# A GLA layer and MLP on one core: units of their own for the last tiles of x, the rows of r brought back at once, x1 and the out weights loaded behind them

## The chip, the cores and the metric

The kernel runs on one core of a Trainium2 chip. The metric is the device time of one execution in microseconds (us). The core has five engines that run side by side and wait for each other by semaphores: PE (TensorE, matrix products), DVE (VectorE), ACT (ScalarE), POOL (GpSimd) and SP (SyncE), which here only issues transfers between the memory and the core (DMA). Each engine, and SP's queue of transfers, takes its instructions in order.

## The reference

With DEPTH = 1 only the first layer is run: gated linear attention (GLA) and an MLP, on 1024 tokens of 1024 numbers.

```python
x = x + gla_mixer(rms_norm(x, norm_mix), w_in, w_gk_up, b_gk, g_onorm, w_out)
x = x + sqrelu_mlp(rms_norm(x, norm_ffn), w_ff1, w_ff2)
return rms_norm(x, final_norm)

def gla_mixer(h, ...):
    q, k, v, r, gk_low = split(h @ w_in)
    log_a = log_sigmoid(gk_low @ w_gk_up + b_gk) / 16
    # per head and chunk of tokens: a state S, decayed by exp(cumsum(log_a))
    #   o = (q * exp(b)) @ S + tril(q k^T decayed) @ v ;  S = decay * S + k_dec^T v
    o = rms_norm(o, g_onorm)
    return (o * silu(r)) @ w_out
```

## The kernel before

Every float32 number is split in a high and a low part, and every product is done as three matmuls (`mm3`). The large products (x by the weights of q and k, of v, of r; the gated outputs by w_out; the MLP's two) go by Strassen's scheme in Winograd's form: seven half-size products ("steps", n = 0 to 6) of sums of 512x512 blocks instead of eight, 48 matmuls each.

The stage that matters is the one behind the q, k, v and r products: a loop over c = 0 to 7, the eight chunks of 128 tokens. PE's order is written out by hand (`manual_schedule`); ACT, DVE, POOL and SP get theirs from a planner that simulates the program and puts in all semaphores. For PE an iteration c is: the operands of chunk c+1 (`operands`, L618), one part of r's last products (`r_part`, L769), the chunk's outputs (`outputs`, L681), its contribution to the state (`new_state`, L652), and the transposes of the previous chunk's gated outputs (`outputs_T`, L709). Between outputs and transposes ACT and DVE normalise and gate the chunk (squares at L696, scale by the rows of r at L705).

r's product has two of its seven steps (n = 1 and 3, `R_LAST`) left out of the large stage for tokens 512 to 1023. They are done here instead, as eight parts `R_PARTS` = (4,1), (4,3), (5,1), ... (7,3), part c in iteration c, 12 matmuls each. The first of a token tile's two parts takes a new bank of PSUM (`rbank`), the second goes on in it. Each part needs:

- the split weights `wr[n]`, made once (L833) and kept in four `big` tiles;
- one tile of split x, 512 KB, brought back from the DRAM copy `xv` by `load_xt` (L755) in two transfers of 256 KB;
- the row tile `rr[t]` with the part of r that is already there. The r stage writes it to the DRAM tensor `rw` (L747, from staging tiles in `raw` and `g4`); `load_r` (L764) brings it back. DVE adds the part (L780), then ACT and DVE apply silu (L725 to L728).

Tiles come from pools with a fixed number of buffers. A new tile takes a buffer that is free, or waits for one. Those that are touched: `big` (8 buffers of 8 KB a partition), `raw` (2 of 4 KB), `wb` (4 of 4 KB), `vx` (8 of 4 KB). `wb` holds weight units in the large stages; in the chunk loop the split rows of v (`v_split`, L640, two tiles a chunk, free when `new_state` of that chunk is done) and the x tiles of `load_xt`. `raw` holds staging in the r stage (its last use there is step n = 4), nothing in the chunk loop, and sums for the out product behind it. `vx` holds v until `v_split`, then x1 (the residual) and one block of w_out.

Behind the loop comes the product with w_out: `from_out` (L904) loads its four blocks, each of two units of 512 KB (block 11 into `vx`, 21 into `wb`, 12 and 22 into `wa`); `load_x1` (L927) loads eight tiles of x, onto which the products are added (`onto_x1`, L931, DVE at L935). In the code before, x1's loads wait for v's last rows to be written (`last_v`), and the w_out loads for nothing but buffers.

`order_after(..., wait=False)` only tells the planner to put one instruction behind another; on one queue that costs no semaphore. `run(True)` (`general`) is a second form of the program for other inputs; it is behind a branch that is not taken here.

Of the kernel before, what the change touches and what calls it, by code (L numbers as in the profile page):

```python
# [8 lines left out]
F32 = mybir.dt.float32  # L9
F32R = mybir.dt.float32r  # L10
# [6 lines left out]
P = 128  # L17
T = 1024
# [22 lines left out]
def order_after(tc, inst, other, wait=True):  # L41

    kind = mybir.DependencyClass.Sync if wait else mybir.DependencyClass.NoSync
    tc.add_manual_dep(inst.ins, other.ins.name, mybir.DependencyInfo(kind, mybir.DependencyReason.DATA),
                      reason="order of phases")
# [3 lines left out]
def hybrid_trunk(ctx: ExitStack, tc: tile.TileContext, x, xT, w_head, w_r, w_gk, w_up,  # L49
                 w_out, w_ff1, w_ff2, vecs, g_fin, out):  # L50
    nc = tc.nc
# [8 lines left out]
    def new(tag, dtype=F32):  # L60
        count[0] += 1
        pool_ = ps if tag in ("mm", "gl") else sb
        return pool_.tile(SHAPE.get(tag, [P, 1024]), dtype, tag=tag, bufs=BUFS[tag], name=f"{tag}{count[0]}")
# [4 lines left out]
    def mm(o, w, m, start, stop, partial=False):  # L68

        pe.matmul(o, w, m, start=start, stop=stop, skip_group_check=partial)  # L70
# [48 lines left out]
    def run(general):  # L119
# [8 lines left out]
        def half(hf):  # L128
            return slice(hf * 512, hf * 512 + 512)
# [12 lines left out]
        R_FIRST, R_LAST = (0, 5, 2, 4, 6), (1, 3)  # L142
# [287 lines left out]
        box = {}  # L430
# [187 lines left out]
        def operands(c, bank_tag="gl"):  # L618

            ah, kd = (new("wa", F32R) for _ in range(2))  # L620
            hs, ls = slice(0, 512), slice(512, 1024)
            if general:
                for pair in range(2):
                    src = at_general[c // 4, pair].rearrange("p (h c t) -> p h c t", h=2, c=4)[:, :, c % 4, :]
                    split(two(ah[:, hs], pair), two(ah[:, ls], pair), src)
            else:
                dp = new(bank_tag)
                for h in range(H):
                    kc, qc = (qk_view(n, h)[:, c * P:c * P + P] for n in (1, 0))
                    mm(dp[:, h * P:(h + 1) * P], kc, qc, True, True)  # L630
                at = new("at")
                dve.tensor_tensor(chunks(at), chunks(dp), bc(cmask, [P, 4, P]), op=ALU.mult)
                split(ah[:, hs], ah[:, ls], at)
            kp = new(bank_tag)
            for h in range(H):
                pe.transpose(kp[:, h * P:(h + 1) * P], qk_view(1, h)[:, c * P:c * P + P], ident)  # L636
            split(kd[:, hs], kd[:, ls], kp)
            ops_c[c] = ah, kd

        def v_split(c):  # L640

            vh = [new("wb", F32R) for _ in range(2)]
            for pair in range(2):
                split(vh[pair][:, 0:512], vh[pair][:, 512:1024], v[c][:, half(pair)])
            v[c] = vh
# [35 lines left out]
        def outputs(c):  # L681

            ah = ops_c[c][0]
            S = state.get("S")
            on, st = new("g4"), new("st")
            ss, y, m, t2 = (st[:, 4 * n:4 * n + 4] for n in range(4))
            o = [new("gl") for _ in range(2)]
            for h in range(H):
                d = o[h // 2][:, (h % 2) * DV:(h % 2) * DV + DV]
                mm3(d, *hl_of(ah, h, P), *hl_of(v[c][h // 2], h % 2, DV), True, c == 0)  # L690
                if c:
                    mm(d, qk_view(0, h)[:, c * P:c * P + P], S[:, h * DV:h * DV + DV], False, True)
            with tc.high_priority():
                for h in range(H):
                    vs = slice(h * DV, h * DV + DV)
                    act.activation(on[:, vs], o[h // 2][:, (h % 2) * DV:(h % 2) * DV + DV], AF.Square, accum_out=ss[:, h:h + 1])  # L696
                act.activation(y, ss, AF.Ln, scale=r_ss[:, c:c + 1], bias=eps)
                act.activation(y, y, AF.Exp, scale=-0.5)
                dve.tensor_scalar(m, ss, r_ss[:, c:c + 1], EPS, op0=ALU.mult, op1=ALU.add)
                dve.tensor_tensor(t2, y, y, op=ALU.mult)  # L700
                dve.scalar_tensor_tensor(t2, t2, -0.5, m, op0=ALU.mult, op1=ALU.mult)
                dve.scalar_tensor_tensor(y, t2, 1.5, y, op0=ALU.add, op1=ALU.mult)
                for h in range(H):
                    vs = slice(h * DV, h * DV + DV)
                    dve.scalar_tensor_tensor(on[:, vs], o[h // 2][:, (h % 2) * DV:(h % 2) * DV + DV], y[:, h:h + 1],  # L705
                                             rr[c][:, vs], op0=ALU.mult, op1=ALU.mult)
            normed_o[c] = on
# [12 lines left out]
        rr, rbank, xt_, wr, stage = {}, {}, {}, {}, {}  # L720
# [33 lines left out]

        def load_xt(t, n):  # L755

            u = new("wb", F32R)
            u3 = u.rearrange("p (k c) -> p k c", c=P)
            for kh in range(2):
                src = xv[n][kh].rearrange("p (k t) -> p k t", t=512)  # L760
                nc.sync.dma_start(u3[:, 4 * kh:4 * kh + 4, :].bitcast(F32), src[:, :, (t % 4) * P:(t % 4) * P + P])
            xt_[t, n] = u3

        def load_r(t):  # L764

            rr[t] = new("big")
            nc.sync.dma_start(rr[t][:, 0:T], rw[t])

        def r_part(t, n):  # L769

            if n == R_LAST[0]:
                rbank[t] = new("mm")
            u, p_ = xt_.pop((t, n)), rbank[t]
            for kp in range(4):
                w = wr[n][kp // 2][:, kp % 2]
                mm3(p_, u[:, 2 * kp, :], u[:, 2 * kp + 1, :], w[:, 0, :], w[:, 1, :], n == R_LAST[0] and kp == 0,
                    n == R_LAST[1] and kp == 3, True)
            d = rr[t][:, half(int(PART[n][0]) - 1)]
            with tc.high_priority():
                dve.tensor_tensor(d, p_, d, op=ALU.add)  # L780
            silu(t, d, d, rr[t][:, T:T + 512])
# [48 lines left out]
        def r_last():  # L830

            for n in R_LAST:
                wr[n] = wR.split(n)  # L833
                load_xt(4, n)
            load_r(4)

        fine_steps.add((0, 0))
# [23 lines left out]
        last_v = box["v"]  # L861


        load_r(0)
        v_split(0)
        R_PARTS = [(t, n) for t in range(4, TT) for n in R_LAST]
        if not general:
            v_split(1)
        for c in range(TT):
            if c == 4 and not general:  # L870

                over = new("st")
                dve.tensor_reduce(over[:, 0:1], top, axis=mybir.AxisListType.X, op=ALU.max)
                dve.tensor_scalar(over[:, 1:2], over[:, 0:1], RANGE, None, op0=ALU.is_gt)
                pf = new("gl")
                mm(pf[:, 0:1], ones, over[:, 1:2], True, True)
                dve.tensor_copy(flag, pf[:, 0:1])
            more = c + 1 < TT
            if general:
                if c % 4 == 0:  # L880
                    for h in range(H):
                        prep_general(h, c // 4)
                operands(c)
                if c:
                    v_split(c)
            elif more:
                operands(c + 1, "mm")
                if c:
                    v_split(c + 1)
            if more:  # L890
                if c:
                    load_xt(*R_PARTS[c + 1])
                if c + 1 < 4:
                    load_r(c + 1)
                if R_PARTS[c + 1][1] == R_LAST[0]:
                    load_r(R_PARTS[c + 1][0])
            r_part(*R_PARTS[c])
            outputs(c)
            if more:
                new_state(c)  # L900
            if c:
                outputs_T(c - 1)

        def from_out(a, b, kh, dst):  # L904

            nc.sync.dma_start(dst.rearrange("p (h n) -> p h n", h=2),
                              w_out[4 * b + 2 * a:4 * b + 2 * a + 2, :, half(kh)].rearrange("h p n -> p h n"))

        def from_up(c):
            def bring(a, b, kh, dst):  # L910
# [14 lines left out]
        x1 = {}  # L925

        def load_x1(t):  # L927
            x1[t] = new("vx")
            order_after(tc, nc.sync.dma_start(x1[t], x[t * P:(t + 1) * P, :]), last_v)

        def onto_x1(n, lane, p_):  # L931
            e, dh = int(PART[n][0]) - 1, int(PART[n][1]) - 1
# [6 lines left out]

        so = Side(True, {f"{a}{b}": og_block(a, b) for a in (1, 2) for b in (1, 2)}, dve, pair_temp, late=True)  # L940
        wo = weight_side(False, from_out, dve, "vx")
        wo.load("11")
        wo.load("21")
        ops = [[so.split(0), wo.split(0)]]
        for t in range(4):
            load_x1(t)
        wo.load("12")
        wo.load("22")
        for t in range(4, 8):
            load_x1(t)  # L950
# [197 lines left out]
```

## Time and profile before

| | us |
|---|---|
| median of three runs | 1015.25 |
| the three runs | 1014.17, 1015.25, 1015.42 |
| the profiled execution | 1014.16 |
| its span | 1012.4 |
| mean granted clock of PE | 0.994 |

Times in the profile count from the start of the span; the span is 1.76 us shorter than the execution's own time. A row of a timeline gives start, duration (both us), engine, line, operation, output<-inputs, size, how many were merged, and in brackets how long the engine was idle before and what released it. PE is matmuls, PEld their weight loads, SPq the issuing of transfers by SP. A row of waits gives the total in us, how often, and the longest. A row of stretches gives length, then busy time (and count) of PE, PEld, DVE, ACT and POOL, the clock granted to PE, the DMA engines' busy share and GB/s. A row of transfers gives the count, the size of one and the median us from issue to landing. The chunk loop lies between about 227 and 308 us.

### The profile page before, as it was taken

Reading aid. Unit: us, or ns where it says so; the run is one execution under the profiler, and the core shown is the slowest. Engines: PE = TensorE matmul, PEld = TensorE weight load, DVE = VectorE, ACT = ScalarE, POOL = GpSimd, SP = SyncE. Lnnn points to the kernel's source line nnn. Section 1 sums busy time; section 2 is a strip of 40 time slices with the busy share of each in tenths; the row PEclk is TensorE's granted clock in tenths of the full one; section 3 lists DMA queues with packets and bytes.
Section 4 is the critical chain, followed back from the end, with each engine's and each line's share of the span. In section 5 each row is a group of like instructions: output and inputs, shape, how many; then the busy total and the mean of one; then the engine's idle time right before and its main releaser. Section 6 shows DMA issues by size and latency. Waiting matters only on the chain.

```text
span 1012.4 us, 12293 instructions
## 1 busy us (share of the span) xinstructions
PE 993.0 (98%) x4572; PEld 829.0 (82%) x4572; DVE 738.3 (73%) x899; ACT 555.9 (55%) x842; POOL 225.1 (22%) x142
## 2 busy tenths in 40 slices
PE   9999999999989999999999999999999999999995
PEld 8888878888878888888888888888888888888884
DVE  6994786868889998979964339965339965339965
ACT  7776555778775378667332446332446332446355
POOL 0000110113430000042224241224241224241270
PEclk9999999999999999999999999999999999999998
DMA  9899794576462224772224951124861124860004
GB/s 281 313 328 371 268 308 181 214 254 204 160 203 89 63 63 187 277 274 73 62 63 167 343 237 43 54 72 166 317 262 46 49 76 166 331 235 16 1 1 170
DMA packets 98957, 176.87 MB, mean 175 GB/s; under 512 B 5576, under 2 KB 67144, under 8 KB 87368
## 3 DMA queue, kind: packets, MB, share of 16 engines
q1 hardware_dynamic: 98328, 175.59, 48.9%
q8 instruction: 38, 0.62, 0.2%
q10 hardware_dynamic: 560, 0.40, 0.1%
q14 instruction: 31, 0.25, 0.1%
HBM read 138.23 MB, written 37.75 MB: 174 GB/s over the span
## 4 chain that ended last, share of the span: by engine, by line
PE 81%; DMA 2%; ACT 1%; DVE 1%; issue 1%; ACTq 0%; DVEq 0%
PE gl L70 54%; PE mm L70 26%; DMA wb<-xv 2%; PE mm L970 1%; DVE vx L935 0%; ACT g L1040 0%; PE mm L636 0%; PE mm L715 0%; ACT hq L717 0%; ACT st L1041 0%; ACT g L696 0%; DVE st L1044 0%; ACT big L81 0%; ACT st L1042 0%; DVE g L1048 0%
## 5 line engine op out<-in xcount | busy, mean ns | idle before, releaser
L70 PE MATMUL gl<-big,big 128*128 128x512 f32 x2712 | 631.3, 390 | 0.0
L70 PEld LDWEIGHTS gl<-big,big 128*128 128x128 f32 x2712 | 508.4, 188 | 105.1 <-DVE big L82 0.4
L70 PE MATMUL mm<-big,big 128*128 128x512 f32 x1224 | 288.2, 389 | 0.0
L70 PEld LDWEIGHTS mm<-big,big 128*128 128x128 f32 x1224 | 229.8, 188 | 47.7
L82 DVE TENSOR_TENSOR big<-wa,big 128x1024 fp32r<-128x1024 f32 (+1 forms) x120 | 162.0, 1376 | 105.4 <-ACT big L81 105.3
L81 ACT ACTIVATE big<-wa 128x1024 fp32r<-128x1024 f32 (+1 forms) x120 | 120.7, 1039 | 134.7 <-PE gl L70 64.0
L184 POOL TENSOR_TENSOR wa<-wa,wa 128x1024 f32<-128x1024 f32 x28 | 75.2, 2690 | 160.5 <-DVE big L82 159.6
L184 POOL TENSOR_TENSOR wa<-wa,wb 128x1024 f32<-128x1024 f32 x14 | 42.9, 3065 | 283.1 <-DVE big L82 283.1
L82 DVE TENSOR_TENSOR big<-wb,big 128x1024 fp32r<-128x1024 f32 x48 | 63.5, 1339 | 52.8 <-ACT big L81 50.6
L82 DVE TENSOR_TENSOR big<-hq,big 128x1024 fp32r<-128x1024 f32 x48 | 61.3, 1283 | 42.8 <-ACT big L81 42.8
L81 ACT ACTIVATE big<-wb 128x1024 fp32r<-128x1024 f32 x48 | 49.1, 1052 | 64.8 <-PE mm L70 31.0
L81 ACT ACTIVATE big<-hq 128x1024 fp32r<-128x1024 f32 x48 | 48.6, 1053 | 61.4 <-PE gl L70 32.4
L81 ACT ACTIVATE big<-raw 128x1024 fp32r<-128x1024 f32 x42 | 43.6, 1058 | 52.1 <-DVE raw L184 25.2
L82 DVE TENSOR_TENSOR big<-raw,big 128x1024 fp32r<-128x1024 f32 x42 | 66.8, 1607 | 2.3 <-ACT big L81 2.2
L935 DVE TENSOR_TENSOR vx<-gl,vx 128x512 f32<-128x512 f32 x95 | 63.2, 682 | 3.5 <-PE gl L70 3.2
L184 POOL TENSOR_TENSOR wa<-wb,wa 128x1024 f32<-128x1024 f32 x14 | 41.1, 2947 | 44.7 <-DVE big L82 44.7
L556 POOL COPY top<-g 128x4 f32<-128x4 f32 x8 | 8.5, 1066 | 179.7 <-DVE g L548 179.7
L993 ACT ACTIVATE hq<-hq 128x1024 f32<-128x1024 f32 x24 | 25.4, 1058 | 29.6 <-DVE hq L986 29.6
L678 POOL TENSOR_SCALAR g<-g,est 128x256 f32<-128x256 f32 x28 | 28.7, 1039 | 57.0 <-DVE g L675 37.8
L70 PE MATMUL gl<-wb,wa 128*128 128x256 f32 x180 | 32.5, 312 | 0.0
L70 PE MATMUL mm<-big,wb 128*128 128x512 f32 x96 | 25.3, 414 | 6.4 <-DMA wb<-xv 5.8
L935 DVE TENSOR_TENSOR vx<-mm,vx 128x512 f32<-128x512 f32 x45 | 29.8, 681 | 1.4 <-PE mm L70 1.4
(191 smaller groups left out, 834.0 us busy)
## 6 DMA issues: line engine op xcount, KB each, us to landing
big<-xw SPq DMA_DIRECT2D x42, 1024.0 KB, 6.8
big<-xv SPq DMA_DIRECT2D x20, 1024.0 KB, 5.7
xv<-big SPq DMA_DIRECT2D x14, 1024.0 KB, 8.1
xw<-big SPq DMA_DIRECT2D x14, 1024.0 KB, 5.5
wb<-in_w_ff SPq DMA_DIRECT2D x32, 256.0 KB, 3.3
wa<-in_w_ff SPq DMA_DIRECT2D x32, 256.0 KB, 3.7
wa<-in_w_ff SPq DMA_DIRECT2D x16, 512.0 KB, 4.6
wb<-in_w_ff SPq DMA_DIRECT2D x16, 512.0 KB, 4.5
```

What stands on the lines that cost most here:

```text
L70: pe.matmul(o, w, m, start=start, stop=stop, skip_group_check=partial)
L81: last["split"] = act.activation(hi, src, AF.Copy)
L82: last["low"] = dve.tensor_tensor(lo, src, f32(hi), op=ALU.subtract)
L184: op = self.eng.tensor_tensor(*(self.ap(b, kp, 2) for b in (o, x_, y_)), op=op)
L556: pool.tensor_copy(top[:, 8 * h + 4 * hf:8 * h + 4 * hf + 4].unsqueeze(2), a[:, :, P - 1:P])
L678: pool.tensor_scalar(S[:, vs], Z[:, vs], g, None, op0=ALU.mult)
L935: return dve.tensor_tensor(xd, p_, xd, op=ALU.add)
L970: pe.transpose(p_[:, c * P:(c + 1) * P], xn[4 * hf + c][:, kt * P:(kt + 1) * P], ident)
L993: act.activation(d2, d2, AF.Relu)
```

## The change

The x tiles get `raw`'s two buffers instead of `wb`'s. The rows of tokens 0 to 511 share two `big` tiles and are all brought back before the loop, the row of tile 5 with them; those of tiles 6 and 7 follow in iterations 2 and 4. The loads of w_out are put behind the load of part 6's x tile, and those of x1 behind part 7's, without a semaphore; x1's wait for v is gone.

```diff
         def load_xt(t, n):
-            u = new("wb", F32R)
+            u = new("raw", F32R)
...
-                nc.sync.dma_start(u3[:, 4 * kh:4 * kh + 4, :].bitcast(F32), src[:, :, (t % 4) * P:(t % 4) * P + P])
+                box["xt", t, n] = nc.sync.dma_start(u3[:, 4 * kh:4 * kh + 4, :].bitcast(F32),
+                                                    src[:, :, (t % 4) * P:(t % 4) * P + P])
...
         def load_r(t):
-            rr[t] = new("big")
+            if t >= 4 or t % 2 == 0:
+                box["rr"] = new("big")
+            rr[t] = box["rr"] if t >= 4 else box["rr"][:, (t % 2) * T:(t % 2) * T + T]
             nc.sync.dma_start(rr[t][:, 0:T], rw[t])
...
             for n in R_LAST:
                 wr[n] = wR.split(n)
-                load_xt(4, n)
+                if n == R_LAST[0] or not general:
+                    load_xt(4, n)
             load_r(4)
...
-        load_r(0)
+        for t in range(4):
+            load_r(t)
+        load_r(5)
         v_split(0)
...
             if more:
-                if c:
+                if c or general:
                     load_xt(*R_PARTS[c + 1])
-                if c + 1 < 4:
-                    load_r(c + 1)
-                if R_PARTS[c + 1][1] == R_LAST[0]:
-                    load_r(R_PARTS[c + 1][0])
+                if c in (2, 4):
+                    load_r(5 + c // 2)
             r_part(*R_PARTS[c])
...
         def from_out(a, b, kh, dst):
-            nc.sync.dma_start(dst.rearrange("p (h n) -> p h n", h=2),
+            load = nc.sync.dma_start(dst.rearrange("p (h n) -> p h n", h=2),
                               w_out[4 * b + 2 * a:4 * b + 2 * a + 2, :, half(kh)].rearrange("h p n -> p h n"))
+            order_after(tc, load, box["xt", 7, R_LAST[0]], wait=False)
...
         def load_x1(t):
             x1[t] = new("vx")
-            order_after(tc, nc.sync.dma_start(x1[t], x[t * P:(t + 1) * P, :]), last_v)
+            order_after(tc, nc.sync.dma_start(x1[t], x[t * P:(t + 1) * P, :]), box["xt", 7, R_LAST[1]], wait=False)
```

## The prediction

> **What bounds the kernel now.** I begin with the page's busy line and the list of what TensorE (PE) waited for, cut to the stage that the change touches (225 to 320 us).
>
> ```profile
> PE 993.0 (98%) x4572; PEld 829.0 (82%) x4572; DVE 738.3 (73%) x899; ACT 555.9 (55%) x842; POOL 225.1 (22%) x142
> ```
>
> ```profile
> PE mm L70 <- DMA wb<-xv: 5.8, 4, 2.8
> PE mm L70 <- ACT hq L717: 0.5, 1, 0.5
> ```
>
> PE is the bound: it is idle for 1012.4 - 993.0 = 19.4 us of the span. Here it waits 5.8 us, in four waits, for a load of x tiles. The timeline of PE shows where; these are all the gaps that it marks from 205 to 312 us:
>
> ```profile
> 245.70 2.96 PE L70 MATMUL mm<-big,wb 128*128 128x512 f32 x12 [0.86 <-DMA wb<-xv]
> 256.42 3.04 PE L70 MATMUL mm<-big,wb 128*128 128x512 f32 x12 [0.98 <-DMA wb<-xv]
> 277.67 3.03 PE L70 MATMUL mm<-big,wb 128*128 128x512 f32 x12 [1.15 <-DMA wb<-xv]
> 287.95 3.02 PE L70 MATMUL mm<-big,wb 128*128 128x512 f32 x12 [0.46 <-ACT hq L717]
> 299.26 4.19 PE L70 MATMUL mm<-big,wb 128*128 128x512 f32 x12 [2.85 <-DMA wb<-xv]
> ```
>
> Each row is a call of r_part (12 matmuls): parts 2, 3, 5, 6 and 7. Part 7 took 4.19 us instead of 3.03. The view by stretches says why (PE busy first, granted clock third from the end), and that behind this stage PE has no gap:
>
> ```profile
> 299.30:301.00 1.70, 1.70 (x7) 1.44 (x8) 1.70 (x3) 0.07 (x1) 1.21 (x1) 0.93 1.03 375
> 301.00:303.00 2.00, 2.00 (x6) 1.51 (x6) 0.92 (x3) 0.99 (x1) 0.00 (x0) 0.50 0.69 217
> 303.00:305.00 2.00, 2.00 (x11) 1.85 (x10) 1.51 (x4) 1.51 (x2) 0.00 (x0) 0.71 0.71 209
> ...
> 500.00:600.00 100.00, 100.00 (x442) 82.82 (x442) 49.20 (x51) 37.29 (x42) 33.26 (x12) 1.00 0.51 187
> ```
>
> Behind the 2.85 us gap the clock falls to half. Lost: 1.70*0.07 + 2.00*0.50 + 2.00*0.29 = 1.70 us. So an instant won here reaches the end, as long as the engines that feed PE keep up.
>
> Why are the loads late? The SP queue, in order of time:
>
> ```profile
> 211.95 3.77 SPq L747 DMA_DIRECT2D rw<-raw  x4
> ...
> 240.75 0.32 SPq L767 DMA_DIRECT2D big<-rw  x1
> 241.95 1.20 SPq L761 DMA_DIRECT2D wb<-xv  x2
> ...
> 284.59 1.20 SPq L761 DMA_DIRECT2D wb<-xv  x2
> 285.84 8.24 SPq L906 DMA_DIRECT2D wa<-in_w_out  x4
> 294.86 1.20 SPq L761 DMA_DIRECT2D wb<-xv  x2
> ```
>
> and its own waits, and the page's time to landing:
>
> ```profile
> SPq L767 <- DVE g L705: 14.5, 4, 4.8
> ...
> SPq L761 <- PE gl L70: 6.3, 6, 1.5
> ```
>
> ```profile
> wb<-xv SPq DMA_DIRECT2D x16, 256.0 KB, 4.1
> ...
> vx<-in_x SPq DMA_DIRECT2D x8, 512.0 KB, 3.9
> ...
> rw<-raw SPq DMA_DIRECT2D x8, 256.0 KB, 3.6
> ```
>
> A tile is issued at 241.95 and used at 245.70: the transfer lies bare between its issue and its matmuls. It was issued late because its buffer is one of the four of wb, which the split rows of v hold until the chunk's state products end (L761 waits for PE gl), and because the queue stood behind row loads that wait for L705. Part 7's load also stands behind four loads of out weights, which kept the queue for 8.24 us.
>
> **The change part by part.**
> *x tiles in raw.* No instruction is added; 16 loads get other buffers. A tile of part c now frees when part c-2 ends. That is one whole chunk ahead: part 3's could be issued when part 1 ends, near 238 us (part 1's row stands below), against 256.42 when it is used, with 4.1 us to land. Parts 3, 5 and 7 use a bank that they already hold, so nothing else is due in front of them: 0.98 + 1.15 + 2.85 = 4.98 us go, and with the last the 1.70 us of clock.
>
> Part 2 opens a new bank, as part 6 did, which started once ACT's L717 had emptied the transposes. For part 2:
>
> ```profile
> 244.44 0.86 ACT L717 ACTIVATE hq<-gl,vec 128x256 f32<-128x256 f32 x2
> ```
>
> That ends at 245.30, and the start was 245.70. The gain is between 0.40 (this row decides, as at part 6) and 0.86 (the bank came free earlier); I take 0.40, nearest to part 6. Part 6 keeps its 0.46: 0 to 0.46 to win, I take 0.
>
> The Trainium skill ("TensorE: Matmul & The Clock Gate", Part 1) says that the clock halves after an idle window of about 3.4 us. Our gap is 2.85 us; taken by the letter it would not cause the fall, the 1.70 us would stay, and the gain would be 1.70 less. I go by the rows, since the fall follows the longest gap and none of the others.
>
> *The first two tiles.* raw is held by staged rows until they are written out: issued from 211.95 to 215.72 and landed 3.6 us later, so free by 219.3. The tiles land 4.1 us later, by 224, and parts 0 and 1 start here:
>
> ```profile
> 228.09 3.02 PE L70 MATMUL mm<-big,wb 128*128 128x512 f32 x12
> ...
> 235.06 3.00 PE L70 MATMUL mm<-big,wb 128*128 128x512 f32 x12
> ```
>
> Cover of 4 us: cost 0. Without it each us late is a us of PE.
>
> *wb for v alone.* v can be split two chunks ahead. It moves ACT and DVE work forward; gain on the path 0, since no gap was put down to it.
>
> *Rows at once.* Eight loads as before, same bytes. Rows 0 to 3 sit in two tiles, so nothing waits for a chunk's L705 until row 6; that removes most of the queue's 14.5 us. Off PE's path: 0 by itself, it lets the x tiles go. Row 7 still waits for chunk 3's L705, with part 6's load behind it; that load is then issued near 267.5 and used after 280. Cost 0.
>
> *Out weights behind part 6's load, x1 behind part 7's.* No new wait on a semaphore, but an order in SP. Part 7's tile frees near 277.7 (part 5 ends at 280.70, less about 3 us won by then). By the first use of x1 it, up to six x1 tiles and three of the four weight blocks (two units each) have to come, 13 times 512 KB or 6.8 MB. That use:
>
> ```profile
> 311.08 0.68 DVE L935 TENSOR_TENSOR vx<-gl,vx 128x512 f32<-128x512 f32 x1
> ```
>
> which moves to about 304. 6.8 MB in 26 us is 262 GB/s, between these two (last number):
>
> ```profile
> 284.50:299.30 14.80, 11.49 (x80) 10.33 (x78) 13.84 (x30) 13.08 (x35) 7.24 (x8) 1.00 0.76 249
> ...
> 296.00:298.00 2.00, 0.42 (x4) 0.18 (x2) 2.00 (x7) 2.00 (x6) 1.75 (x2) 1.00 1.07 376
> ```
>
> So it fits, narrowly. Cost 0, with an upper end in the rivals.
>
> *What is late next: DVE.* The first of those two rows shows DVE busy 13.84 of 14.80 us (its busy time is the fourth number). With part 7 no longer held up, PE wants chunk 6's transposes sooner, and they need its L705:
>
> ```profile
> 295.82 0.60 PE L715 MATMUL gl<-ident,g 128*128 128x128 f32 x4
> ...
> 298.29 1.42 DVE L82 TENSOR_TENSOR big<-vx,big 128x1024 fp32r<-128x1024 f32 x1
> ...
> 299.71 1.42 DVE L184 TENSOR_TENSOR wa<-wa,vx 128x1024 f32<-128x1024 f32 x1
> 301.06 0.86 DVE L705 SCALAR_TENSOR_TENSOR g<-gl,st,big 128x256 f32<-128x256 f32 x2
> 303.49 0.69 DVE L780 TENSOR_TENSOR big<-mm,big 128x512 f32<-128x512 f32 x1 [1.57 <-PE mm L70]
> 304.10 0.87 DVE L705 SCALAR_TENSOR_TENSOR g<-gl,st,big 128x256 f32<-128x256 f32 x2
> ```
>
> PE is through with its earlier transposes at 296.42. L705 ends at 304.97; without DVE's 1.57 us behind PE, 303.40: 6.98 us later. PE has part 7 (3.03) and chunk 7's outputs between, as long as chunk 5's:
>
> ```profile
> 280.54 0.52 PE L70 MATMUL gl<-wb,wa 128*128 128x256 f32 x3
> ...
> 283.50 1.79 PE L70 MATMUL gl<-wb,wa 128*128 128x256 f32 x12
> ```
>
> 2.96 us, together 5.99. So PE would wait about 1.0 us in DVE's present order; 0 if L82 and L184 (2.84 us) come behind L705, 2 if one more such tile comes before it. I take 1.0.
>
> Then chunk 7's L705, which must free a bank for the out step's fourth lane:
>
> ```profile
> 307.61 11.17 PE L70 MATMUL gl<-big,big 128*128 128x512 f32 x48
> ...
> 314.69 1.65 DVE L705 SCALAR_TENSOR_TENSOR g<-gl,st,big 128x256 f32<-128x256 f32 x4
> ```
>
> The fourth lane starts three quarters of 10.9 us in, at 315.8; half of L705 is done at 315.5. A slack of 0.3 us, and DVE will have some 4 us less time ahead of it. Cost 0 to 2, by one filler of 1.2 us or two; I take 0.8.
>
> **Sum:** 0.40 + 4.98 + 1.70 - 1.0 - 0.8 = 5.3 us off. The profiled execution took 1014.16 us (span 1012.4 and 1.76 around it); the timed runs were 1014.17, 1015.25 and 1015.42. The middle of the four is 1014.7, so 1009.4 us. The ends: at best 5.84 + 0.46 + 1.70 = 8.0 off, 1006.7; with DVE's worst (4 us) 3.1 off, 1011.6.
>
> **The rivals.**
> *A. DVE becomes the bound at the hand-over.* It may pay more than 4 us: chunk 6's and 7's evacuations wait behind splits and sums, PE stops over 2.8 us at once, and the clock falls again (1.70). For it: DVE is 94% busy there. Against: over the whole stage it is not, 67.96 of 82.60 us, so the earlier chunks can take work off it:
>
> ```profile
> 225.00:307.60 82.60, 76.16 (x483) 68.46 (x482) 67.96 (x146) 63.41 (x162) 28.66 (x28) 0.98 0.58 187
> ```
>
>  The gain is 7.1 less 4 to 6.5: 1011.6 to 1014.
> *B. Nothing to be seen.* The waits for x tiles go but part 2, 3, 5, 7 stand for ACT's or DVE's splits of wa just as long, or the planner's new order of ACT and DVE costs it. Against: no gap but part 6's names them. 1013 to 1015.5.
> *C. Slower: x1 behind weights.* One mechanism: SP works in order. A load of x1 put behind the last pair of weights in wb (free only when chunk 6's state products end), lands late; DVE, in order too, stops at the first L935, the banks of the out step stay full, and PE stops. It decides from the point where x1's first tile lands after 304; it makes the kernel slower when it lands more than 5.3 us later, with a clock fall after 2.8. The first x1 landing at 313 gives 9 + 1.7 - 5.3 = 5.4 us more: 1020. Against: by 277.7 five buffers of vx are empty, and planning puts what is ready first.
> *D. It does not do what it says:* the tiles in raw come late instead, because SP waits with them for staged rows. That hits parts 0 and 1 only, and 4 us cover them.
>
> *E. The clock falls all the same*, at its own time and not for the gap: the 1.70 us stay, 1011.1. Against: no other stretch from 225 to 299 us is below 1.00. That is the skill's rule taken by the letter.
>
> **How the numbers follow.** What a measurement of this kernel can tell from no change is about 0.2%, 2 us: faster means below 1013.2, slower above 1017.3. The forecast (1006.5 to 1011.6) has 0.66, of which 0.06 is E; A 0.15, of which 0.12 still counts as faster; B and D 0.10, of which 0.02 is faster and 0.08 the same; C 0.09, slower. Faster 0.80, same 0.11, slower 0.09. The range 1006.5 to 1013.8 leaves out C and most of B.
>
> **What would show it.** Right: no wait of PE for raw<-xv; x tiles issued before 240 and landed some us before use; clock 1.00 from 225 to 310; chunk 6's transposes the first PE gap of the hand-over, with DVE L705 as its releaser. Wrong: PE gaps put down to ACT or DVE at the parts; an SP row of x1 later than 300; a gap of over 2.8 us anywhere from 290 to 330; any change ahead of 205 us.

## The result, and the profile after

The changed kernel takes 1005.16 us (median of 4 runs, 1004.96 to 1006.05), against 1015.34 for the kernel before in the same measurement (median of 4 runs; three lie between 1014.17 and 1015.42, one at 1019.37). The ratio is 0.9895, 95% interval 0.9867 to 0.9922; it is taken over all runs, here and below, and need not be that of the medians (0.9900 here). It is faster by 1%, about twice the forecast 5.3 us, and below the low end of the range (1006.5). The profiled execution took 1004.96 us, its span is 1003.7.

The busy line of the page, and then all that PE waited for in the whole program:

```profile
PE 991.0 (99%) x4572; PEld 827.3 (82%) x4572; DVE 737.1 (73%) x899; ACT 554.6 (55%) x842; POOL 226.0 (23%) x142
```

```profile
PE gl L70 <- DVE ones L90: 1.1, 1, 1.1
PE mm L70 <- DVE vx L483: 0.8, 1, 0.8
PE gl L70 <- DVE big L82: 0.3, 1, 0.3
```

No wait for a tile of x is left, and none for ACT: all three lie outside the chunk loop. The eight parts and the out step on PE's timeline (rows between them left out) have no gap marked:

```profile
228.35 3.02 PE L70 MATMUL mm<-big,raw 128*128 128x512 f32 x12
235.33 3.00 PE L70 MATMUL mm<-big,raw 128*128 128x512 f32 x12
...
244.89 3.01 PE L70 MATMUL mm<-big,raw 128*128 128x512 f32 x12
...
254.72 2.98 PE L70 MATMUL mm<-big,raw 128*128 128x512 f32 x12
...
264.63 3.01 PE L70 MATMUL mm<-big,raw 128*128 128x512 f32 x12
...
274.45 2.98 PE L70 MATMUL mm<-big,raw 128*128 128x512 f32 x12
...
283.97 3.01 PE L70 MATMUL mm<-big,raw 128*128 128x512 f32 x12
...
292.18 2.98 PE L70 MATMUL mm<-big,raw 128*128 128x512 f32 x12
299.68 11.18 PE L70 MATMUL gl<-big,big 128*128 128x512 f32 x48
```

From part 0 to the out step it is 71.33 us; before it was 307.61 - 228.09 = 79.52. I call this the loop's time; it is 8.19 us shorter. By the stretches between neighbouring starts the savings are, in us:

| from part to part | before | after | saved |
|---|---|---|---|
| 0 to 1 | 6.97 | 6.98 | -0.01 |
| 1 to 2 | 10.64 | 9.56 | 1.08 |
| 2 to 3 | 10.72 | 9.83 | 0.89 |
| 3 to 4 | 10.18 | 9.91 | 0.27 |
| 4 to 5 | 11.07 | 9.82 | 1.25 |
| 5 to 6 | 10.28 | 9.52 | 0.76 |
| 6 to 7 | 11.31 | 8.21 | 3.10 |
| 7 to out step | 8.35 | 7.50 | 0.85 |

SP's queue shows why (same columns as before; a row merges neighbouring transfers, and its start is that of the first):

```profile
234.43 14.03 SPq L761 DMA_DIRECT2D raw<-xv  x5
248.57 0.55 SPq L770 DMA_DIRECT2D big<-rw  x1
249.16 19.70 SPq L761 DMA_DIRECT2D raw<-xv  x5
268.91 0.62 SPq L770 DMA_DIRECT2D big<-rw  x1
269.58 0.94 SPq L910 DMA_DIRECT2D vx<-in_w_out  x2
277.46 1.21 SPq L761 DMA_DIRECT2D raw<-xv  x2
278.72 3.49 SPq L934 DMA_DIRECT2D vx<-in_x  x4
```

Part 2's tile is issued from 234.43 and used at 244.89; part 7's at 277.46, used at 292.18. Issue and use now lie more than 10 us apart, where they were 3.75 us apart for part 2. The clock and the rate over the stage:

```profile
225.00:308.00 83.00, 82.75 (x521) 74.23 (x521) 73.09 (x158) 65.83 (x173) 29.12 (x28) 1.00 0.61 204
```

### The profile page after: what moved, and what is told of

Its sections match the earlier page's. It is cut to its first block, busy times and chain, and to the rows that moved or that the text cites. A ratio compares the mean times of both kernels' runs of the same rounds, so it can differ in the third digit from the quotient of the medians.

```text
span 1003.7 us, 12278 instructions
## 1 busy us (share of the span) xinstructions
PE 991.0 (99%) x4572; PEld 827.3 (82%) x4572; DVE 737.1 (73%) x899; ACT 554.6 (55%) x842; POOL 226.0 (23%) x142
## 4 chain that ended last, share of the span: by engine, by line
PE 81%; ACT 2%; DVE 2%; issue 1%; ACTq 0%; DVEq 0%
PE gl L70 54%; PE mm L70 26%; PE mm L975 1%; PE mm L636 0%; ACT g L696 0%; DVE vx L940 0%; PE mm L715 0%; DVE big L82 0%; ACT wb L81 0%; DVE big L783 0%; ACT g L1045 0%; PE gl L715 0%; DVE g L705 0%; DVE g L675 0%; ACT hq L717 0%
## 5 line engine op out<-in xcount | busy, mean ns | idle before, releaser
L989 ACT ACTIVATE hq<-gl 128x512 f32<-128x512 f32 x36 | 21.3, 592 | 14.6 <-PE gl L70 14.6
```

The costliest lines, as they stand in the source:

```text
L989: act.activation(d, p_, AF.Copy)
```

## The experiments

The loop's time is taken from each run's own trace, from part 0's start to the out step's. A profile is one execution.

**Which part of the change does it.** Four kernels, each with a part left out or alone. Only the new units (the kernel before with one word changed):

```diff
-            u = new("wb", F32R)
+            u = new("raw", F32R)
```

> Only the x tiles move from wb to raw; rows, out weights and x1 as before. If the units of their own carry the gain: all six bare transfers (parts 2 to 7) are covered, no PE wait for raw<-xv, the out step starts 7 to 8.2 us earlier than the 307.6 us of before, total 7 to 9 us less. If the rows standing in front of them in SP's queue matter as much: the loads behind a row load that waits for L705 (parts 2, 3, 4, 6) stay late, with PE waits of about 1 us each, and 3 to 5 us are won.

Measured: 1006.72 us (ratio 0.9919, interval 0.9902 to 0.9935), loop 299.55 - 228.24 = 71.31 us. No wait for x tiles.

The change without the new units:

```diff
-            u = new("raw", F32R)
+            u = new("wb", F32R)
```

> The change without its new units: x tiles stay in wb, rows at once, out weights behind part 6's load, x1 behind part 7's. If the buffers are the cause: each load still waits for the state products that free wb, gaps of 0.9 to 2.9 us at parts 2 to 7 stay, the clock falls again, 0 to 1.5 us are won. If the queue was the cause: most gaps go and 3 us or more are won.

Measured: 1012.78 us (ratio 0.9981, interval 0.9972 to 0.9991), loop 305.68 - 228.74 = 76.94 us. PE's gaps in its trace:

```profile
245.96 3.00 PE L70 MATMUL mm<-big,wb 128*128 128x512 f32 x12 [0.47 <-ACT hq L717]
256.00 3.06 PE L70 MATMUL mm<-big,wb 128*128 128x512 f32 x12 [0.27 <-DMA wb<-xv]
286.40 3.43 PE L70 MATMUL mm<-big,wb 128*128 128x512 f32 x12 [0.48 <-ACT hq L717]
298.94 2.97 PE L70 MATMUL mm<-big,wb 128*128 128x512 f32 x12 [3.66 <-DMA wb<-xv]
```

One gap went (part 5's), two shrank (parts 2 and 3), part 6's stayed and part 7's grew. With the rows out of the way the queue is somewhat better, but each load still waits for wb: SP stood 34.4 us in six waits before these loads for PE's products, and part 7's is issued at 293.72. The clock did not fall in this execution, which alone makes 1.7 us of the 2.6 saved in the loop; it was also the fastest of its ten (1010.97 us), so the loop of a middling one is probably longer. Neither expectation came as it was put: 2.4 us were won by the medians, 1.9 by the ratio, and in the profiles 1.3 us of the gain lie behind the last matmul (below).

Rows one by one again, and then later loads ordered as before, each with the rest of the change:

```diff
-            if t >= 4 or t % 2 == 0:
-                box["rr"] = new("big")
-            rr[t] = box["rr"] if t >= 4 else box["rr"][:, (t % 2) * T:(t % 2) * T + T]
+            rr[t] = new("big")
...
-        for t in range(4):
-            load_r(t)
-        load_r(5)
+        load_r(0)
...
-                if c in (2, 4):
-                    load_r(5 + c // 2)
+                if c + 1 < 4:
+                    load_r(c + 1)
+                if R_PARTS[c + 1][1] == R_LAST[0]:
+                    load_r(R_PARTS[c + 1][0])
```

> Units of their own and the order of out weights and x1, but the rows loaded one by one as before. If rows at once are only tidiness: within 0.5 us of the changed kernel in the trace, no PE wait for raw<-xv. If they matter: the loads behind a row load come late, waits of 0.5 to 1.5 us at two or more parts, 2 us or more lost against the changed kernel.

```diff
-            order_after(tc, load, box["xt", 7, R_LAST[0]], wait=False)
...
-            order_after(tc, nc.sync.dma_start(x1[t], x[t * P:(t + 1) * P, :]), box["xt", 7, R_LAST[1]], wait=False)
+            order_after(tc, nc.sync.dma_start(x1[t], x[t * P:(t + 1) * P, :]), last_v)
```

> Units of their own and rows at once, but out weights and x1 ordered as before. If the order of the later loads matters: part 7's load again stands behind out weights that wait for wa, a gap of 1 to 3 us at part 7 with a fall of the clock, 3 to 5 us lost against the changed kernel. If not: part 7's load, free one chunk earlier, is ahead of them by itself and the trace is within 0.5 us of the changed kernel.

Measured: 1006.83 us (0.992, interval 0.9904 to 0.9937) and 1006.33 us (0.9914, interval 0.9897 to 0.993); the loop is 71.33 us in both. Neither has a wait for x tiles. So inside the loop the units carry everything, and neither the rows nor the order adds anything to them. No run gives wb two more buffers instead: whether the tiles need units of their own, or only two buffers more, is not told apart.

**The changed kernel once more, with more rounds.**

> The changed kernel once more, with more rounds. If the change is worth what the trace shows inside the chunk loop (8.2 us there, 7.9 us at the end of the last matmul): 7.5 to 9.2 us, a ratio of 0.991 to 0.9925, and the rest of the first 10.2 us was the spread of the runs of before. If something outside the loop came with it: 10 us again, a ratio of 0.990 or less.

Measured: 1005.49 us (ratio 0.991, interval 0.9894 to 0.9926): 9.8 us less by the medians, 9.1 by the ratio; the loop is 300.12 - 228.69 = 71.43 us. The ratio does not tell the two expectations apart, since its interval holds both. The profiles do: something outside the loop came with the change. The table has, in us, the loop, the time from the last matmul's end to the end of the span, and two things that the trace records of SP: the longest stop inside the 20 instructions that go ahead of its last one, and how many instructions SP has.

```
kernel            loop    last matmul to end   SP's stop   SP's instructions
before            79.52   11.06                1.30        565
before_b          78.73   11.05                1.25        565
before_c          79.76   11.16                1.38        565
xt_only           71.31   11.11                1.35        563
part6_raw         76.38   11.16                1.43        565
xt_order          71.33   10.89                1.01        561
xt_rows           71.33   10.86                1.04        562
rows_order        76.94    9.76                none        560
after             71.33   10.16                none        560
after_again       71.43   10.52                none        560
gate_first        70.58    9.91                none        560
gap_small         72.86    9.73                none        556
gap_large         75.15    9.74                none        555
v_later           70.47    9.86                none        560
```

Every kernel with both the rows at once and the new order has 9.7 to 10.5, every other one 10.9 to 11.2. This is 0.3 to 1.4 us, behind all matmuls and behind the last output (issued at 1005.21 before, 997.34 after). There SP goes through a list of instructions, nearly all on semaphores. In the seven runs of the first group it stands still once inside that list, for 1.0 to 1.4 us; in the seven of the second it does not, though four of them wait longer before the very last instruction (0.6 to 1.1 us, where it is 0.42 in all others). Counted to the end of the execution, behind the span, the groups lie further apart: 12.6 to 12.9 us against 11.4 to 11.8. The stop goes with the number of SP's instructions, 561 or more against 560 or fewer, and the page's count of packets on the instruction queue q14 goes with it too (31 or 32 against 30). That SP waits there for its next instructions is a guess that fits; no run changes the number alone.

**The kernel before, profiled twice more.** The source is the same.

> The kernel before, profiled a second time. If its first profile is typical: 79.5 us from part 0's start to the out step, a gap of about 2.9 us at part 7 and a fall of the clock behind it. If the fall is a matter of chance: the same gaps, but 77.8 us and granted clock 1.00 right through, or 1.7 us more with a second fall.

> The kernel before, profiled a third time: as for the second. The start up to part 0, and the stretch from the last matmul to the end of the span, tell how much the runs spread outside the chunk loop; if the surplus of the medians (10 us against 8.2 in the loop) is spread, these two vary by about 1 us between the profiles of one kernel.

Measured: 1013.93 and 1014.86 us; loops 307.40 - 228.67 = 78.73 and 308.21 - 228.45 = 79.76 us. Each had one fall of the clock behind part 7's gap, so the first profile was typical. The gaps differ by up to 0.8 us from one execution to the next (part 3's: 0.98, 0.78 and 1.60). Outside the loop the three profiles spread less than 1 us: part 0 starts at 228.09, 228.67 and 228.45, and the stretch behind the last matmul is 11.05 to 11.16. Part 6 in the third profile:

```profile
288.48 2.96 PE L70 MATMUL mm<-big,wb 128*128 128x512 f32 x12 [0.56 <-DMA wb<-xv]
```

The gap that two profiles put down to ACT's L717 is put down to the transfer in this one.

**Whose wait was part 6's?** The kernel before, with one tile in raw:

```diff
-            u = new("wb", F32R)
+            u = new("raw" if (t, n) == (7, R_LAST[0]) else "wb", F32R)
```

> The kernel before with one x tile, part 6's, in raw. If part 6 waited for its transfer and the profile named the wrong releaser: it starts right behind its operands, the 0.46 us gap goes and parts 5 to 6 take 9.5 to 9.9 us instead of 10.28. If it waited for ACT's L717 as the profile says: a gap of 0.3 us or more stays there with the same releaser.

Measured: 1011.83 us. PE and ACT there (the operands end at 287.52):

```profile
286.92 0.60 PE L636 MATMUL mm<-ident,hq 128*128 128x128 f32 x4
287.27 1.41 PE L70 MATMUL mm<-big,raw 128*128 128x512 f32 x5
```

```profile
287.05 0.86 ACT L717 ACTIVATE hq<-gl,vec 128x256 f32<-128x256 f32 x2
```

Part 6 starts 0.64 us before that copy of L717 ends (287.91), so it does not need it; what it waited for in the kernel before was its transfer. Parts 5 to 6 take 287.27 - 277.73 = 9.54 us, as after the change (9.52). In the first profile the two ends lie side by side. The copy is

```profile
287.00 0.85 ACT L717 ACTIVATE hq<-gl,vec 128x256 f32<-128x256 f32 x2
```

and ends at 287.85; the first half of the tile landed at 287.81, by the last update of its semaphore in the trace, and part 6 started at 287.95.

**Does the clock fall for the gap?** The changed kernel with part 7's load held back, behind PE's last matmul of chunk 6's outputs, and then of its state products (`late` is set for this load alone, and its call at the usual place is left out; shown for the outputs):

```diff
+                if late:
+                    order_after(tc, box["xt", t, n], last["pe"])
...
             outputs(c)
+            if c == 6 and not general:
+                load_xt(*R_PARTS[7], late=True)
             if more:
                 new_state(c)
```

> The changed kernel with part 7's load held until chunk 6's outputs are done on PE, so that PE has to wait for it by some 1.5 to 2.5 us. If the clock falls only behind a gap near 2.8 us or longer: granted clock 1.00 right through, and the loss is the gap alone. If any gap over the 1.15 us seen before does it: 0.50 for about 3.4 us behind it, 1.7 us more lost.

> The same with the load held until chunk 6's state products are done: a gap of some 3.5 to 5 us. If the fall of the clock belongs to the gap: 0.50 for about 3.4 us behind it and about 1.7 us lost besides the gap. If the fall before was a matter of its own time and not of the gap: 1.00 right through.

Measured: 1006.76 and 1009.17 us, one run each; loops 301.46 - 228.60 = 72.86 and 303.65 - 228.50 = 75.15 us. Part 7 in the two:

```profile
294.60 3.08 PE L70 MATMUL mm<-big,raw 128*128 128x512 f32 x12 [1.92 <-DVE big L728]
```

```profile
295.30 4.58 PE L70 MATMUL mm<-big,raw 128*128 128x512 f32 x12 [2.66 <-DMA raw<-xv]
```

The first is put down to DVE's L728, but the load, issued at 290.40, landed its first half at 294.46, just ahead of the start at 294.60. The second gap came out shorter than expected, but the clock fell behind it. The clock column (third from the end) of that run, and of rows_order behind its gap of 3.66 us:

```profile
294.00:295.90 1.90, 0.60 (x3) 0.54 (x4) 1.90 (x4) 0.26 (x1) 1.90 (x3) 0.99 0.82 225
295.90:297.00 1.10, 1.10 (x4) 0.90 (x3) 1.10 (x3) 0.00 (x0) 0.83 (x1) 0.50 0.86 212
297.00:299.20 2.20, 2.20 (x6) 1.66 (x5) 1.15 (x3) 1.06 (x1) 0.00 (x0) 0.50 0.99 364
```

```profile
297.00:299.20 2.20, 0.26 (x1) 0.29 (x2) 2.20 (x5) 0.44 (x2) 2.20 (x2) 1.00 1.10 338
299.20:301.00 1.80, 1.80 (x9) 1.48 (x9) 1.58 (x3) 0.41 (x1) 0.17 (x1) 1.00 1.02 402
```

A gap of 2.66 us has a fall, one of 3.66 us has none: length alone does not decide. The last section has what does.

**DVE's order at the hand-over.** In the changed kernel two splits stand ahead of chunk 6's gating on DVE, and PE's transposes are stretched, here DVE and then PE:

```profile
294.30 1.42 DVE L82 TENSOR_TENSOR big<-vx,big 128x1024 fp32r<-128x1024 f32 x1
295.65 0.68 DVE L783 TENSOR_TENSOR big<-mm,big 128x512 f32<-128x512 f32 x1
296.25 0.15 DVE L702 SCALAR_TENSOR_TENSOR st<-st 128x4 f32<-128x4 f32 x1
296.32 1.22 DVE L82 TENSOR_TENSOR big<-hq,big 128x1024 fp32r<-128x1024 f32 x1
297.45 1.65 DVE L705 SCALAR_TENSOR_TENSOR g<-gl,st,big 128x256 f32<-128x256 f32 x4
```

```profile
298.14 1.34 PE L715 MATMUL mm<-ident,g 128*128 128x128 f32 x4
```

The experiment puts the first of the two behind L705 (`box["gated", 6]` is the last L705 of chunk 6):

```diff
         ops = [[so.split(0), wo.split(0)]]
+        order_after(tc, last["low"], box["gated", 6], wait=False)
```

> The changed kernel with DVE's order altered at one place: the low half of the out weights' second split comes behind chunk 6's gating (L705) instead of ahead of it. If DVE's order is what holds chunk 6's transposes (they take 1.34 us there instead of 0.60): the time from part 7's start to the out step falls from 7.50 to 6.7 to 6.9 us, and the out step starts 0.6 to 0.8 us earlier. If not: 7.50 stays, or the out step's fourth lane waits for its bank instead and nothing is won.

Measured: 1004.52 us (ratio 0.9899, interval 0.9882 to 0.9915), 1.0 us below the changed kernel in the same measurement (1005.49; the runs of the two do not overlap). Part 7 to the out step is 299.43 - 292.68 = 6.75 us, and the transposes take their 0.60 us:

```profile
298.64 0.60 PE L715 MATMUL mm<-ident,g 128*128 128x128 f32 x4
```

DVE ahead of the gating and in it:

```profile
295.09 1.21 DVE L184 TENSOR_TENSOR wa<-wa,vx 128x1024 f32<-128x1024 f32 x1
296.22 0.68 DVE L783 TENSOR_TENSOR big<-mm,big 128x512 f32<-128x512 f32 x1
296.82 1.64 DVE L705 SCALAR_TENSOR_TENSOR g<-gl,st,big 128x256 f32<-128x256 f32 x4
```

The second split also went behind L705, and a sum of 1.21 us came ahead of it: so 1.42 + 1.22 - 1.21 = 1.43 us less stand there. The 0.75 us came out as expected.

**The copies on ACT.** On top of that, the split of v behind the copies of the transposes on ACT; it is called at the end of the iteration, with an edge (`box["turned", 0]` is such a copy):

```diff
                 split(vh[pair][:, 0:512], vh[pair][:, 512:1024], v[c][:, half(pair)])
+                if c > 1 and not general:
+                    order_after(tc, last["split"], box["turned", 0], wait=False)
...
                 operands(c + 1, "mm")
-                if c:
-                    v_split(c + 1)
...
             if c:
                 outputs_T(c - 1)
+                if more and not general:
+                    v_split(c + 1)
```

> gate_first with the split of v behind the copies of the transposes (L717) on ACT, where it stood ahead of them in the chunks. If those copies are what is left of PE's waits in the loop: iterations 2 to 5 fall from 9.8-9.9 us to about 9.5, the out step starts 0.6 to 1.2 us earlier than with gate_first, about 1003.7 us. If the split of v is needed at once: outputs wait for wb and the loop gets longer, 1005 us or more.

Measured: 1003.81 us (ratio 0.9896, interval 0.988 to 0.9913). The time looks like the first expectation's, but the kernel before took 1013.84 in this measurement, against 1015.25 in that of gate_first, and the ratio is gate_first's. The loop is 299.53 - 229.06 = 70.47 us. Parts 2 to 5 are 9.72, 9.76 and 9.52 us apart, 0.1 to 0.3 less each than after the change, and one of the three came to the 9.5 that was expected; so the copies were a part of what was left there, and not shown to be all of it. But chunk 7's v is then late, which the second expectation had:

```profile
295.61 0.50 PE L70 MATMUL gl<-wb,wa 128*128 128x256 f32 x2 [0.19 <-DVE wb L82]
```

Part 7 to the out step takes 7.21 us, 0.46 more than in gate_first. What is won in the chunks is lost at the hand-over.

## Why the prediction was wrong in size

The direction and the mechanism held: the x tiles waited for wb, and the gaps and the fall of the clock went with them. What failed were sizes, three terms of the sum and one that was missing, all to the same side. Up to the start of the out step the sum had 6.1 us (its 5.3, and the 0.8 that it gave back behind that), and 8.19 came.

- **Parts 2 and 6** were the largest error: 0.40 and 0 us against 1.08 and 0.76, together 1.44 us. The step was "this row decides, as at part 6": I took the profile's releaser at part 6, L717, for the true one, and carried it over to part 2. part6_raw shows that PE did not wait for that copy. The profile names what came last by its records, and the copy ended 0.04 us behind the landing of the transfer's first half; the transfer (issued at 284.59, used at 287.95) fitted as well, and I had its row.
- **The bank of the fourth lane**, 0.8 us, was not paid at all. The out step takes 11.18 us after the change and 11.17 before. Chunk 7's gating moved forward by more than PE did: its last L705 ends 6.85 us behind the start of the out step (306.53), where it was 8.73 (316.34). The forecast gave DVE less time ahead of it, not more.
- **The marked gaps** add up to less than the bare transfers cost here: the stretches up to parts 3, 4, 5 and 7 got 5.51 us shorter, with 4.98 us of gaps marked. Half of the difference is part 4 (0.27), which had no mark in the first profile, and 0.26 us in the second; part 3's stretch won 0.09 less than its mark.
- **Chunk 6's transposes** were the one term of DVE that came as worked out: with the clock's 1.70 us won, the stretch from part 7 to the out step would be 6.65 us (rows_order, without a fall, has 6.74); it is 7.50, so 0.85 us were given back, against 1.0 forecast. gate_first shows that DVE's order is the cause. Rival A, that DVE takes over 4 us, fell, though from chunk 6's outputs to the out step DVE is busy 12.65 of 12.87 us:

```profile
286.81:299.68 12.87, 12.74 (x82) 11.17 (x80) 12.65 (x25) 12.29 (x33) 4.26 (x4) 1.00 0.99 359
```

- **The clock's 1.70 us** went with part 7's gap; rival E fell. But the reason I gave, the longest gap, was not the right one (last section).
- **Costs put at 0** held: the first two tiles were covered (parts 0 and 1 as before), and x1 and the out weights came in time; DVE's first addition to x1 is at 303.68, against the 304 worked out. Rival C did not come about: four tiles of x1 go out right behind part 7's load, at 278.72. Rivals B and D fell by the same rows.
- **Outside the loop** I had no term. The two profiled executions, 1014.16 and 1004.96 us, differ by 9.20 us: 7.88 up to the end of the last matmul (the loop's 8.19, less a start that was 0.26 us later and 0.05 in between), 0.91 behind it and 0.41 outside the span (1012.44 and 1003.66). These 1.3 us go with SP's list at the end; why it stops there stays open. The medians' 9.8 and 10.2 us hold 0.6 to 1.0 more, which I could not assign; the executions of the kernel before spread from 1011.37 to 1019.37 us.

## What to carry to other kernels

A transfer that is issued just before its use shows as several waits with different releasers; when one engine's wait ends within a landing time of a bare transfer's issue, price it as the transfer too, whoever is named (here part 6, and part 7 of gap_small). When a buffer is shared between a long user and a prefetch, giving the prefetch two buffers of its own was here worth the whole gain in the loop, and tidying the queue in front of it added nothing to that. A hand-over between stages is worth a look at the order of the feeding engine: with 1.43 us less ahead of the gating on DVE, the loop got 0.75 us shorter.

## What the runs showed of the hardware

The trace records each change of PE's granted clock. In all fourteen runs the changes lie whole multiples of 3.413 us behind the first record, and the falls behind part 7's gap last 3.413 us. In the kernel before, the first record is at 7.21 and the fall at 300.75, which is 86 times 3.413 us later; so a window runs from 297.34 to 300.75, and part 7's gap (296.41 to 299.26) has 0.93 us ahead of it and 1.92 in it. With the gap of part 7 laid on each run's grid, the idle time in us inside single windows is:

```
kernel       gap    idle in the two windows it touches    clock
before_c     3.00   2.92, 0.08                            falls at the end of the first
gap_large    2.66   2.66                                  falls at its end
before_b     2.63   2.12, 0.51                            falls at the end of the first
before       2.85   0.93, 1.92                            falls at the end of the second
rows_order   3.66   1.88, 1.78                            stays
part6_raw    2.69   0.92, 1.77                            stays
gap_small    1.92   0.55, 1.37                            stays
```

In these seven runs the clock falls where PE is idle 1.92 us or more inside one window, and stays where it is idle 1.88 us or less in each (by the modelled ends of the matmuls). The ends of the programs agree: the window in which the last matmul ended had 2.52, 2.90, 3.02 and 3.07 us of idle time in before, xt_only, after and v_later, and the clock fell at its end; in the ten others it had at most 1.88 us (after_again), and the clock fell one window later. So the same gap may or may not cost 1.7 us, by where it lies: 3.66 us cut in two halves cost nothing more, 2.63 us did. The Trainium skill ("TensorE: Matmul & The Clock Gate", Part 1) has the window of 3413 ns that runs freely, and the records agree with it. It asks for a whole idle window, and there the runs differ: somewhat over half of one was enough.
